# Strassen pairs of a decoder layer: the accumulating DMAs take their second operand from DRAM

## The chip, the cores and the metric

The kernel runs on one core of a Trainium2 chip. Its time is the device time of one execution in microseconds (us); several runs are given as their median. A core has five engines that run side by side: TensorE (PE, with its weight loads PEld), VectorE (DVE), ScalarE (ACT), GpSimd (POOL) and SyncE (SP). SP issues the loads from DRAM here and POOL the accumulating DMAs; both kinds of transfer are carried out by the same 16 DMA engines.

## What is computed

One decoder layer on 256 tokens of width 2048, in float32: a feed-forward half step, a mixer (dilated attention beside gated linear attention), cross-attention to 256 memory tokens, and a second feed-forward half step. The change touches only the two half steps, each of which is

```python
def swiglu(h, w_gate, w_up, w_down):
    return (jax.nn.silu(h @ w_gate) * (h @ w_up)) @ w_down

x = x + 0.5 * swiglu(rms_norm(x, ffn1_norm[l]), ffn1_w_gate[l], ffn1_w_up[l], ffn1_w_down[l])
```

with `w_gate` and `w_up` of 2048 x 5632 and `w_down` of 5632 x 2048. Before it reaches the core, each weight is packed as `W[c, g]`: column block `c` of 512 columns, row group `g` of 512 rows, laid out as a tile of 128 partitions x 4 x 512 (1 MB, 8 KB in a row per partition).

## The kernel before

**Exact products from a split.** Each weight tile `raw` is split into a rounded part `wh` (a cast on ScalarE, L136) and a rest `wl` (a subtraction on VectorE, L137), and so are the activations. A product is three matrix products, `wh` with the high and low part of the activations and `wl` with the high part (`mm3`, L158 to L165; `product`, L188 to L196). `split` is called with the tiles that TensorE will use next, so ScalarE casts, VectorE subtracts and TensorE multiplies, each a tile or two behind the other.

**Half steps.** `ffn` (L346) goes through 11 column blocks `f` in three parts of 4, 4 and 3. Within a part it makes gate and up for each block, then the partial product with `w_down` for all four output columns. The first block of a half step uses the plain `proj`; the other ten use `strassen` (L372), so that the program has 20 calls. The first call of the second and of the third part follows directly on the `w_down` products of the part before; the other calls follow on a gate and up, whose transposition (`turn`, L350, casts at L274, subtractions at L275) is done within the next call.

**A Strassen pair.** `strassen` makes gate and up of a column block together. Its row groups 0 and 1 are the two halves of a 2 x 2 block product of the Strassen-Winograd form, which takes 7 products in place of 8 (each `product` is 12 matrix products on half of the tokens); groups 2 and 3 are plain. The four tiles of groups 0 and 1 are `ral` and `rar` (group `a`, gate and up) and `rbl` and `rbr` (group `b`, gate and up). Sums of them are made in place:

- L229: `ral -> ral + rar` on VectorE (`add`, L210 to L212);
- L230: `rar -> rar + rbr`, an accumulating DMA from POOL (`accumulate`, L214 to L216);
- L235: `ral -> ral + rbr`, so `ral` is now the sum of three, on VectorE;
- L240: `ral -> ral + rbl`, an accumulating DMA once `ral` has been split; the sum of all four is used in the last of the seven products (L252).

In between, `parts` splits the tiles in this order: `ral` as loaded, `ral` with `rar`, `ral` with `rbr` too, `rbl` (L239), `rar` with `rbr` (L241), `rbr` (L244). Then come the left tile of group 2 (`wgroup`, L139), the sum of four in `ral` (L252), and the right tile of group 2, the left and the right one of group 3. ScalarE and VectorE follow that order.

**Buffers and queues.** In the half steps, weight tiles come alternately from two pools of three buffers each (`load`, L121 to L133). A buffer may be written again when every instruction that read the last tile in it is done, and accumulating DMAs count among these. Of the tiles of a call, the left one of group 3 goes to the buffer that `rbr` had, the right one of group 3 to that of `rbl`. All loads are issued from SP, in one fixed order; SP stands still while the next load's buffer isn't free. The load into `rbl`'s buffer is the next one on SP after the right tile of group 2. The framework orders the instructions of each engine at build time, by priority and by when it reckons them ready (`high_priority` moves them ahead) and adds the semaphore waits itself.

Of the kernel before, what the change touches and what calls it, by code (L numbers as in the profile page):

```python
# [49 lines left out]
def layer_kernel(ctx: ExitStack, tc: tile.TileContext, A: dict, out: bass.AP):  # L50
# [23 lines left out]
    def FT(tag, bufs, shape, dt, name):  # L74
        return phase["pool"].tile(shape, dt, tag=tag, name=name, bufs=bufs)

    def W2(shape, name, dt=F32):
        return sp.tile(shape, dt, tag="w", name=name)
# [4 lines left out]
    def PM(shape, name):  # L83
        return pm.tile(shape, F32, tag="ps", name=name)
# [7 lines left out]
    def tick():  # L92
        due = []
        for e in pend:
            e[0] -= 1
            if e[0] <= 0:
                due.append(e)
        for e in due:
            pend.remove(e)
            e[1]()  # L100
# [20 lines left out]
    def load(W, c, g):  # L121

        if wload:
            return wload.pop(0)
        kn, n = W.shape[-2:]
        with tc.high_priority(WPRI):
            phase["loads"] += 1
            if phase["half_step"] and phase["loads"] % 2:
                raw = FT("raw", FRAW, [P, kn, n], F32, "raw")
            else:  # L130
                raw = wp.tile([P, kn, n], F32, tag="raw", name="raw")
            SY.dma_start(raw, W[c, g])
        return raw  # L133

    def split(wh, wl, src):
        SC.copy(wh, src)  # L136
        V.tensor_sub(wl, src, wh.bitcast(F32))  # L137

    def wgroup(W, c, g, fine=None):  # L139

        raw = load(W, c, g)
        n = W.shape[-1]
        kn = W.shape[-2]
        whole = phase["half_step"]
        m = kn if whole else kn // 2
        for h in range(1 if whole else 2):
            with tc.high_priority(WPRI):
                wh, wl = (FT(x, FWB if whole else WB, [P, m, n], F32R, x) for x in ("wh", "wl"))
                for i in range(m if fine else 1):
                    d = slice(i, i + 1) if fine else slice(0, m)  # L150
                    if fine:
                        fine(m * h + i)
                    split(wh[:, d], wl[:, d], raw[:, m * h + d.start:m * h + d.stop])
            ks = [(kn * g + m * h + kk, wh[:, kk], wl[:, kk]) for kk in range(m)]
            for i in range(0, m, kn // 2):
                yield ks[i:i + kn // 2]

    def mm3(acc, lhs, half, first, last, ts=range(TT), seeded=False):  # L158

        for t in ts:  # L160
            for i, (k, wh, wl) in enumerate(half):
                lh, ll = lhs(k, t)
                PE.matmul(acc[t], lh, wh, start=first and i == 0, stop=False, skip_group_check=seeded)  # L163
                PE.matmul(acc[t], lh, wl, start=False, stop=False, skip_group_check=seeded)  # L164
                PE.matmul(acc[t], ll, wh, start=False, stop=last and i == len(half) - 1, skip_group_check=seeded)  # L165
# [22 lines left out]
    def product(acc, lhs, w, start):  # L188

        wh, wl = w  # L190
        first = start
        for i, j, w in ((0, 0, wh), (1, 0, wh), (0, 1, wl)):
            for k in range(4):
                PE.matmul(acc, lhs(k)[i], w[:, k], start=first, stop=j == 1 and k == 3, skip_group_check=not start)  # L194
                first = False
        tick()  # L196

    def strassen(Wl, cl, Wr, cr, lhs, ab, sums, groups):

        a, b = ab  # L200
        ral, rar = load(Wl, cl, a), load(Wr, cr, a)
        rbr, rbl = load(Wr, cr, b), load(Wl, cl, b)

        def parts(src):
            with tc.high_priority(WPRI):
                wh, wl = (FT(x, FWB, [P, 4, 512], F32R, x) for x in ("wh", "wl"))
                split(wh, wl, src)
            return wh, wl

        def add(dst, x, y):  # L210
            with tc.high_priority(WPRI):
                V.tensor_add(dst, x, y)  # L212

        def accumulate(dst, x):  # L214
            with tc.high_priority(WPRI):
                G.dma_start(dst, x, accum_op=ALU.add)  # L216

        def of(g, t):
            return lambda k: lhs(4 * g + k, t)

        def s_(i):
            return lambda k: tuple(x[:, i, k] for x in sums)

        x, y = PM([P, 512], "x"), PM([P, 512], "y")
        c0l, c0r, c1r = (pa.tile([P, 512], F32, tag="acc", name="acc") for _ in range(3))
        product(x, of(a, 0), parts(ral), True)
        with tc.high_priority(WPRI):
            SC.copy(c0l, x)  # L228
        add(ral, ral, rar)  # L229
        accumulate(rar, rbr)  # L230
        product(y, s_(0), parts(ral), True)
        with tc.high_priority(WPRI):
            ys = W2([P, 512], "ys")
            SC.copy(ys, y)
        add(ral, ral, rbr)  # L235
        product(x, s_(1), parts(ral), False)
        with tc.high_priority(WPRI):
            V.tensor_sub(c0r, ys, x)  # L238
        product(c0l, of(b, 0), parts(rbl), False)  # L239
        accumulate(ral, rbl)  # L240
        product(x, s_(2), parts(rar), False)  # L241
        with tc.high_priority(WPRI):
            V.tensor_sub(c1r, ys, x)
        product(c0r, s_(3), parts(rbr), False)  # L244
        accs = ((c0l, x), (c0r, c1r))
        for i, g in enumerate(groups):
            for acc, W, c in zip(accs, (Wl, Wr), (cl, cr)):
                for h, half in enumerate(wgroup(W, c, g)):
                    mm3(acc, lhs, half, False, i == len(groups) - 1 and h == 1, seeded=True)
                    tick()  # L250
                if i == 0 and W is Wl and c == cl:
                    product(x, of(b, 1), parts(ral), False)  # L252
        return accs
# [92 lines left out]
    def ffn(pre, r, after, fine=None, last=False):  # L346
# [18 lines left out]
        for part in PARTS:  # L365
            for f in part:
                if sums is None:
                    gate = proj(wg, f, lhs_x, range(4), fine)
                    if callable(r):
                        r = r()  # L370
                else:
                    gate, upv = strassen(wg, f, wu, f, lhs_x, (0, 1), sums, (2, 3))  # L372
                sg = []
                with tc.high_priority(WPRI):
                    for t in range(TT):
                        s = W2([P, 512], "sg")
                        SC.activation(s, gate[t], AF.Silu, scale=r[:, t:t + 1])
                        sg.append(s)
                if sums is None:
                    upv = proj(wu, f, lhs_x, range(4))  # L380
                hs = []
                with tc.high_priority(WPRI):
                    for t in range(TT):
                        h = W2([P, 512], "h")
                        V.scalar_tensor_tensor(h, upv[t], r[:, t:t + 1], sg[t], op0=ALU.mult, op1=ALU.mult)  # L385
                        hs.append(h)
                later(2, lambda f=f, hs=hs: turn(f, hs))
                if sums is None:
                    sums = tuple(FT(n, 1, [P, 4, 4, P], F32R, n) for n in ("sh", "sl"))
                    with tc.high_priority(WPRI):  # L390
                        sums_of(xT[0], xT[1], lambda i: tuple(p[:, 2 * i:2 * i + 2] for p in sums))
# [643 lines left out]
```

## Time and profile before

| what | value |
|---|---|
| timed runs, median (lowest to highest of 3) | 1957.99 us (1957.59 to 1958.06) |
| profiled execution, span from first to last instruction | 1956.1 us |
| mean granted TensorE clock | 0.995 |
| ACT busy | 988.7 us, 51% |
| loads from DRAM (queue q1) | 370.74 MB, DMA engines busy with them 49.9% of the span |
| accumulating DMAs (queue q0) | 41.95 MB, 10.4% |

The span is the profiled execution's own time; the timed runs take in what lies around it. In rows of the timeline the columns are the start in us, the duration in us, the engine, the line, the operation with output and inputs, the number of instructions merged in the row, and in brackets how long the engine was idle before and what ended that. "SPq" and the DMA rows of POOL are the issuing of a DMA, not its transfer. In a list of waits the columns are the time in total, the number of times, and the longest. In a table of windows they are the stretch, its length, then busy time (and instructions) of PE, PEld, DVE, ACT and POOL, the granted clock, the busy share of the DMA engines and GB/s.

### The profile page before, as it was taken

What the parts mean: (1) busy time and instruction counts of PE and PEld (TensorE: products, weight loads), DVE (VectorE), ACT (ScalarE), POOL (GpSimd) and SP (SyncE); (2) the same over time, 40 slices, a digit from 0 to 9 for tenths busy, and PEclk for the clock granted to TensorE, in tenths of its full rate; (3) what the DMA queues carried; (4) which work ended last, traced back from release to release, by engine and by line L of the source; (5) the groups of instructions that cost most, each with busy time, mean ns of one, the idle gap of its engine ahead of it and who ended that gap; (6) DMA issues with size and microseconds to landing.
All of it is one profiled execution on the core that took longest, in us unless ns stands there. A gap on an engine that the chain in (4) does not pass through costs nothing.

```text
span 1956.1 us, 21465 instructions
## 1 busy us (share of the span) xinstructions
PE 1924.5 (98%) x8760; PEld 1586.4 (81%) x8760; DVE 1270.5 (65%) x1027; ACT 988.7 (51%) x956; POOL 96.1 (5%) x101
## 2 busy tenths in 40 slices
PE   8999999999999999999999999899999999999999
PEld 6888878888878888778888889688887788887887
DVE  6776467775578655546785566777646777457863
ACT  6555345553356446444675446555534555335642
POOL 2000000000000000002230000000000000000000
PEclk9999999999999999999999999999999999999999
DMA  9677547775567725445465554567755777556771
GB/s 368 235 236 258 190 148 264 271 268 192 173 220 237 281 82 186 156 167 191 172 232 207 183 192 151 217 236 233 260 184 146 252 272 274 203 178 215 237 285 59
DMA packets 63294, 416.14 MB, mean 213 GB/s; under 512 B 7099, under 2 KB 8251, under 8 KB 14428
## 3 DMA queue, kind: packets, MB, share of 16 engines
q1 hardware_dynamic: 56284, 370.74, 49.9%
q0 software_dynamic: 5760, 41.95, 10.4%
q10 hardware_dynamic: 1152, 2.10, 0.3%
q8 instruction: 68, 1.11, 0.2%
q14 instruction: 30, 0.25, 0.0%
HBM read 370.72 MB, written 2.10 MB: 191 GB/s over the span
## 4 chain that ended last, share of the span: by engine, by line
PE 74%; DVE 15%; ACT 5%; issue 4%; DMA 1%; POOL 0%; SPq 0%; ACTq 0%; DVEq 0%
PE acc L164 21%; PE acc L165 20%; PE acc L163 20%; DVE wl L137 10%; ACT wh L136 5%; PE x L194 4%; DVE raw L212 4%; PE x L165 1%; PE x L164 1%; PE acc L194 1%; PE x L163 1%; DVE h L385 1%; DMA xr<-in_xT_dram 1%; DVE acc L238 1%; PE y L194 0%
## 5 line engine op out<-in xcount | busy, mean ns | idle before, releaser
L137 DVE TENSOR_TENSOR wl<-raw,wh 128x2048 fp32r<-128x2048 f32 (+2 forms) x487 | 931.5, 1932 | 582.6 <-ACT wh L136 581.8
L136 ACT CAST wh<-raw 128x2048 fp32r<-128x2048 f32 (+2 forms) x487 | 777.0, 1619 | 692.5 <-PE acc L165 503.9
L163 PE MATMUL acc<-wh,xTh 128*128 128x512 f32 x1024 | 402.3, 394 | 16.3 <-ACT wh L136 16.3
L164 PE MATMUL acc<-wl,xTh 128*128 128x512 f32 x1024 | 402.9, 393 | 8.9 <-DVE wl L137 8.9
L165 PE MATMUL acc<-wh,xTl 128*128 128x512 f32 x1024 | 400.5, 391 | 0.0
L163 PE MATMUL acc<-wh,hTh 128*128 128x512 f32 x704 | 274.7, 390 | 0.0
L165 PE MATMUL acc<-wh,hTl 128*128 128x512 f32 x704 | 274.0, 389 | 0.0
L164 PE MATMUL acc<-wl,hTh 128*128 128x512 f32 x704 | 273.9, 389 | 0.0
L163 PEld LDWEIGHTS acc<-wh,xTh 128*128 128x128 f32 x1024 | 192.4, 189 | 59.5 <-ACT wh L136 18.9
L164 PEld LDWEIGHTS acc<-wl,xTh 128*128 128x128 f32 x1024 | 193.3, 189 | 56.9 <-DVE wl L137 17.7
L165 PEld LDWEIGHTS acc<-wh,xTl 128*128 128x128 f32 x1024 | 193.4, 189 | 39.7
L165 PEld LDWEIGHTS acc<-wh,hTl 128*128 128x128 f32 x704 | 132.2, 188 | 27.4
L164 PEld LDWEIGHTS acc<-wl,hTh 128*128 128x128 f32 x704 | 132.2, 188 | 27.2
L163 PEld LDWEIGHTS acc<-wh,hTh 128*128 128x128 f32 x704 | 132.2, 188 | 27.1
L216 POOL DMA_DIRECT2D raw<-raw x40 | 34.6, 864 | 1179.5 <-DVE raw L212 966.9
L212 DVE TENSOR_TENSOR raw<-raw 128x2048 f32<-128x2048 f32 x40 | 91.5, 2288 | 0.7
L165 PE MATMUL x<-wh,xTl 128*128 128x512 f32 x160 | 62.6, 391 | 0.0
L164 PE MATMUL x<-wl,xTh 128*128 128x512 f32 x160 | 62.5, 391 | 0.0
L163 PE MATMUL x<-wh,xTh 128*128 128x512 f32 x160 | 62.4, 390 | 0.0
L228 ACT COPY acc<-x 128x512 f32<-128x512 f32 x20 | 11.4, 571 | 95.6 <-PE x L194 95.6
L396 DVE SCALAR_TENSOR_TENSOR x<-acc,x 128x512 f32<-128x512 f32 x48 | 33.0, 687 | 31.6 <-PE acc L165 31.6
L163 PE MATMUL acc<-wh,mTh 128*128 128x512 f32 x128 | 50.1, 392 | 0.0
(302 smaller groups left out, 1958.9 us busy)
## 6 DMA issues: line engine op xcount, KB each, us to landing
raw<-in_ffn_w_up_dram SPq DMA_DIRECT2D x88, 1024.0 KB, 7.0
raw<-in_ffn_w_down_dram SPq DMA_DIRECT2D x88, 1024.0 KB, 4.9
raw<-in_ffn_w_gate_dram SPq DMA_DIRECT2D x85, 1024.0 KB, 6.9
raw<-in_w_in_dram SPq DMA_DIRECT2D x48, 1024.0 KB, 4.7
raw<-raw POOLq DMA_DIRECT2D x40, 1024.0 KB, 6.9
raw<-in_w_out_dram SPq DMA_DIRECT2D x16, 1024.0 KB, 4.7
raw<-in_xattn_w_k_dram SPq DMA_DIRECT2D x4, 1024.0 KB, 4.8
raw<-in_xattn_w_q_dram SPq DMA_DIRECT2D x4, 1024.0 KB, 5.0
```

The costliest lines, as they stand in the source:

```text
L136: SC.copy(wh, src)
L137: V.tensor_sub(wl, src, wh.bitcast(F32))
L163: PE.matmul(acc[t], lh, wh, start=first and i == 0, stop=False, skip_group_check=seeded)
L164: PE.matmul(acc[t], lh, wl, start=False, stop=False, skip_group_check=seeded)
L165: PE.matmul(acc[t], ll, wh, start=False, stop=last and i == len(half) - 1, skip_group_check=seeded)
L194: PE.matmul(acc, lhs(k)[i], w[:, k], start=first, stop=j == 1 and k == 3, skip_group_check=not start)
L212: V.tensor_add(dst, x, y)
L216: G.dma_start(dst, x, accum_op=ALU.add)
L228: SC.copy(c0l, x)
L238: V.tensor_sub(c0r, ys, x)
L385: V.scalar_tensor_tensor(h, upv[t], r[:, t:t + 1], sg[t], op0=ALU.mult, op1=ALU.mult)
L396: V.scalar_tensor_tensor(xs[c][:, t], acc[t], 0.5, xs[c][:, t], op0=ALU.mult, op1=ALU.add)
```

## The change

The two accumulating DMAs of `strassen` read the second summand from the weight in DRAM, `Wr[cr, b]` and `Wl[cl, b]`. These are the very arrays from which `rbr` and `rbl` were loaded (L202), so that the numbers are the same. The tiles `rbr` and `rbl` are still loaded, as they are split and used in products of their own, and `rbr` in the sum at L235.

```diff
         add(ral, ral, rar)
-        accumulate(rar, rbr)
+        accumulate(rar, Wr[cr, b])
         product(y, s_(0), parts(ral), True)
...
         product(c0l, of(b, 0), parts(rbl), False)
-        accumulate(ral, rbl)
+        accumulate(ral, Wl[cl, b])
         product(x, s_(2), parts(rar), False)
```

## The prediction, made before the changed kernel ran

> **What bounds the kernel now.** I read the page first, then the waits, then the timeline of one Strassen call for each engine.
>
> ```profile
> span 1956.1 us, 21465 instructions
> PE 1924.5 (98%) x8760; PEld 1586.4 (81%) x8760; DVE 1270.5 (65%) x1027; ACT 988.7 (51%) x956; POOL 96.1 (5%) x101
> ...
> raw<-in_w_in_dram SPq DMA_DIRECT2D x48, 1024.0 KB, 4.7
> raw<-raw POOLq DMA_DIRECT2D x40, 1024.0 KB, 6.9
> ```
>
> TensorE has work 98% of the span; 1956.1 - 1924.5 = 31.6 us are all it is idle. An edit that touches only two DMAs per call can gain no more than the part of those 31.6 us that hangs on them. The other rows give the time from issue to landing of 1 MB: 4.7 us for a plain load, 6.9 us for an accumulating DMA, 40 of them in 20 calls of `strassen`.
>
> Who makes TensorE wait, and what the load queue waits for (the list of waits, without and with SP):
>
> ```profile
> PE acc L163 <- ACT wh L136: 16.3, 7, 4.4
> PE acc L164 <- DVE wl L137: 8.9, 18, 3.8
> ...
> SPq L132 <- DMA raw<-raw: 538.8, 20, 27.5
> ```
>
> TensorE waits for the casts and differences of weights, never by name for a DMA. But SP, which issues the weight loads in order, stands once in each of the 20 calls until an accumulating DMA lands. Which one, the timeline of an ordinary call (the one at 300 to 345 us; POOL, SP, DVE, ACT, PE) says:
>
> ```profile
> 314.50 0.85 POOL L216 DMA_DIRECT2D raw<-raw  x1 [31.36 <-DVE raw L212]
> 326.43 0.86 POOL L216 DMA_DIRECT2D raw<-raw  x1 [11.08 <-DVE wl L137]
> ...
> 333.36 0.33 SPq L132 DMA_DIRECT2D raw<-in_ffn_w_up_dram  x1
> 333.79 0.37 SPq L132 DMA_DIRECT2D raw<-in_ffn_w_gate_dram  x1
> ...
> 323.84 4.49 DVE L137 TENSOR_TENSOR wl<-raw,wh 128x2048 fp32r<-128x2048 f32 x2 [2.03 <-ACT wh L136]
> ...
> 333.85 6.69 DVE L137 TENSOR_TENSOR wl<-raw,wh 128x2048 fp32r<-128x2048 f32 x3
> ...
> 325.99 5.53 ACT L136 CAST wh<-raw 128x2048 fp32r<-128x2048 f32 x3
> 331.41 1.07 ACT L274 CAST hTh<-tp 128x512 fp32r<-128x512 f32 x2
> 333.41 3.72 ACT L136 CAST wh<-raw 128x2048 fp32r<-128x2048 f32 x2 [0.93 <-DVE wl L137]
> ...
> 341.35 1.07 PE L194 MATMUL x<-wh,xTh 128*128 128x512 f32 x4
> ...
> 344.07 0.39 PE L163 MATMUL acc<-wh,xTh 128*128 128x512 f32 x1
> ```
>
> The second accumulate (L240, `ral += rbl`) is issued at 326.43 and lands 6.93 us later, at 333.36: at that instant SP issues the next load (into the buffer of `rbl`) and 0.05 us later ScalarE starts the last cast of `ral`. The two casts at 333.41 are that of `ral` and that of the right-hand tile of the next group; TensorE uses them at 341.35 and 344.07. So in an ordinary call the landing has slack. The first accumulate (L230) is issued at 314.50; its result is cast first in the x3 at 325.99, though 314.50 + 6.9 = 321.4: 4.6 us of slack.
>
> In four calls there is none: the first of the second and third part of each feed-forward half. One with its rows, then the waits of TensorE in all four:
>
> ```profile
> 540.85 0.86 POOL L216 DMA_DIRECT2D raw<-raw  x1 [10.66 <-DVE wl L137]
> ...
> 538.26 4.49 DVE L137 TENSOR_TENSOR wl<-raw,wh 128x2048 fp32r<-128x2048 f32 x2 [1.72 <-ACT wh L136]
> ...
> 547.84 0.33 SPq L132 DMA_DIRECT2D raw<-in_ffn_w_up_dram  x1
> ...
> 547.88 3.71 ACT L136 CAST wh<-raw 128x2048 fp32r<-128x2048 f32 x2 [1.94 <-DMA raw<-raw]
> ...
> 293.92 0.73 PE L163 MATMUL acc<-wh,xTh 128*128 128x512 f32 x2 [2.43 <-ACT wh L136]
> ...
> 551.64 0.74 PE L163 MATMUL acc<-wh,xTh 128*128 128x512 f32 x2 [1.59 <-ACT wh L136]
> ...
> 1517.48 0.89 PE L163 MATMUL acc<-wh,xTh 128*128 128x512 f32 x2 [2.42 <-ACT wh L136]
> ...
> 1776.69 0.74 PE L163 MATMUL acc<-wh,xTh 128*128 128x512 f32 x2 [1.50 <-ACT wh L136]
> ```
>
> Here TensorE's fixed order puts the right-hand tile's first product ahead, so it waits at 551.64 for the second of the two casts (547.88 + 3.71 = 551.59), and these wait for the landing. The landing is on TensorE's path four times, with 2.43 + 1.59 + 2.42 + 1.50 = 7.94 us of idle time.
>
> How much a later landing costs can be read from the trace, as two of the four land late already:
>
> ```profile
> 282.29 0.85 POOL L216 DMA_DIRECT2D raw<-raw  x1 [10.66 <-DVE wl L137]
> ...
> 290.12 0.33 SPq L132 DMA_DIRECT2D raw<-in_ffn_w_up_dram  x1
> ...
> 262.50 27.95 SPq L132 DMA_DIRECT2D raw<-in_ffn_w_up_dram  x2
> ```
>
> There it took 290.12 - 282.29 = 7.83 us with 2.43 us of idle, against 6.94 us (540.85 to SP's 547.84, less its 0.05) with 1.59: 0.89 us later, 0.84 us more idle. So 0.94 us of time for each us of delay.
>
> **The change part by part.** Instructions stay: 40 accumulates, the same bytes into the same tiles. Three things move.
>
> (1) *What the accumulates wait for.* They no longer wait for the loads of `rbr` and `rbl`. The waits that end last are others (DVE raw L212, DVE wl L137 in the rows above), so this gives 0. The issue on POOL (0.85 us) has nothing queued behind it in these stages: 0.
>
> (2) *The source.* 40 x 1024 KB = 41.9 MB more are read from HBM. What the transfer itself costs, from the stretches of the accumulate alone and of loads alone:
>
> ```profile
> 326.40:333.40 7.00, 7.00 (x33) 5.77 (x32) 7.00 (x5) 6.08 (x5) 0.86 (x1) 1.00 0.73 150
> ...
> 333.40:341.00 7.60, 7.41 (x33) 5.79 (x32) 7.60 (x5) 3.72 (x2) 0.00 (x0) 1.00 0.86 335
> ```
>
> The last two columns are the share of time that the DMA engines are busy and GB/s. The accumulate keeps them busy 0.73 x 7.00 = 5.1 us for 1.05 MB (150 GB/s x 7.00 us); loads need 0.86 x 7.60 = 6.5 us for 335 x 7.60 = 2.55 MB, 2.6 us for the same size. An accumulate costs the engines twice a load, which is what reading two operands instead of one would cost, wherever they lie. How long it takes from DRAM no row shows. Bounds: 2.6 us, if the DRAM side runs beside the read of the destination as a plain load does; 5.1 + 2.6 = 7.7 us, if the fetch comes on top. I take 5.1, since the cost seems to be one of operands and not of place.
>
> [...]
>
> (3) *What is freed earlier.* This is the part that decides. The buffer of `rbl` is no longer read by the accumulate, so SP's load into it waits only for the difference of `rbl`, the second of the x2 groups: 323.84 + 4.49 = 328.33 in place of 333.36 in the ordinary call, 538.26 + 4.49 = 542.75 in place of 547.84 in the other. SP goes 5 us earlier, and nobody waits for that load: its tile is the last of the call to be cast. The loads behind it wait for other buffers (`rbr`, whose difference ends at about 333.3) and move by 0.4 us. So the early load gains 0. But it now runs beside the second accumulate, where today the DMA engines are left to that alone (150 GB/s in that window is its own 1.05 MB). SP's load is issued 1.9 us after the accumulate. Start and end of a load together take 4.7 - 2.6 = 2.1 us, those of an accumulate 6.9 - 5.1 = 1.8; my estimate is that the starts are 1.0 and 1.4 of these. Then the load's bytes come when about 1.5 of the accumulate's 5.1 us are done and 3.6 us, 70%, remain. If the engines take turns piece by piece, 70% of the load's 2.6 us goes ahead of the accumulate's end: 1.8 us. Bounds: 0, if a transfer once begun is finished first or both run side by side; 2.6, if the whole load passes. I take 1.7, near to taking turns.
>
> *The sum.* The landing comes 1.7 us later in all 20 calls. In 16 it is covered: in the call at 326 us ScalarE would cast `ral` at 335.1 to 337.0 and the next tile to 338.9, needed at 341.35 and 344.07; VectorE's three differences, now back to back to 340.54, would wait 0.9 us after the first and end at 341.4, with the last needed at about 344.3 by the product behind 344.07. That cover holds to a delay of about 4.5 us. In the four calls nothing covers it: 4 x 1.7 x 0.94 = 6.4 us. What is late next there is still the same cast. Against the span 1956.1 + 6.4 = 1962.5; the timed runs have a median of 1957.99, 1.9 us around the span, so 1964.4 us, 0.33% slower.
>
> **The rivals.**
>
> *No cost from sharing (1958).* The accumulate, having begun first, is served first, or the two overlap, or the load is not issued earlier because something else holds it: the change then doesn't do what I read from it. Delay under 1 us, cost under 3.9 us. For it: the engines need not share evenly, and no row here shows a load beside an accumulate. Against: the landing at 290.12 took 7.83 us though SP issued nothing between 262.5 and that landing (the x2 row), so even small other traffic in the DMA engines delays an accumulate.
>
> [...]
>
> *A faster accumulate (1952.6), the other side.* If the read of two operands from one SBUF port is what doubles the cost, a DRAM operand halves the transfer to 2.6 us. Of it 1.5 is done when the load comes; the remaining 1.1 takes turns with 1.1 of the load: 2.2 in place of 3.6, a landing 1.4 us earlier. ScalarE is free for it (1.94 us idle before 547.88), and 4 x 1.4 x 0.94 = 5.3 us come off the 7.94. It decides from a busy time of under about 3.3 us per accumulate (1.5 done, 1.8 left, doubled by the turns: 3.6 as today). Near it stands another order: the instruction order is laid out at build time, and if TensorE's order in the four calls became that of the ordinary ones, most of the 7.94 us would go (about 1951).
>
> *A slower accumulate (about 1979).* At 7.7 us of busy time 80% remains when the load comes, and the landing is 2.6 + 0.8 x 2.6 = 4.7 us late. Four calls: 4 x 4.7 x 0.94 = 18 us; the sixteen others lose the 0.2 us beyond their cover of 4.5, 3 us in all. For it: HBM has to be reached for every piece; against: loads from HBM run at twice the accumulate's rate.
>
> **How the numbers follow.** Forecast (delay 1.05 to 2.6 us, +4 to +10): 0.50. No cost: 0.26. Faster accumulate or other order: 0.15. Slower accumulate: 0.09. A measurement of this kernel tells about 0.2%, 3.9 us, from no change. So faster 0.15, same 0.26, slower 0.59. The likeliest time is 1964.4, its own range 1962 to 1968. The 80% range reaches to the faster accumulate and, above, to 2.6 us of delay with some of the slower transfer: 1952 to 1974; it leaves out most of the slow rival and the far end of the other order.
>
> **What would show it.** Right: SP's load into `rbl`'s buffer issued about 2 us after the second accumulate; that accumulate's landing at 8.3 to 9 us, the first one's still near 6.9; the four idle times of TensorE at 3 to 4 us; nothing new in the sixteen other calls. Wrong: a landing of the first accumulate, which has no load beside it, away from 6.9 (then step 2 fails, by that much); a second landing near 6.9 although the load is early (no sharing); the four idle times gone (another order).

## The result: 16 us slower, half of it through TensorE's clock

| kernel | median | range | ratio to before, 95% interval |
|---|---|---|---|
| before | 1957.79 us | 1957.16 to 1958.06 (4 runs) | |
| changed | 1973.99 us | 1972.54 to 1974.82 (4 runs) | 1.0078 [1.0067, 1.0090] |

The profiled execution of the changed kernel is its fastest run: 1972.54 us, a span of 1970.8 us. The page of its profile (span, busy time, the queue of the accumulating DMAs, and time from issue to landing) and its list of waits:

```profile
span 1970.8 us, 21499 instructions
...
PE 1933.8 (98%) x8760; PEld 1593.3 (81%) x8760; DVE 1272.0 (65%) x1027; ACT 988.0 (50%) x956; POOL 97.9 (5%) x101
...
q0 software_dynamic: 5760, 41.95, 11.6%
...
raw<-in_ffn_w_up_dram POOLq DMA_DIRECT2D x20, 1024.0 KB, 7.9
raw<-in_ffn_w_gate_dram POOLq DMA_DIRECT2D x20, 1024.0 KB, 9.1
...
PE acc L163 <- ACT wh L136: 22.4, 7, 3.9
...
SPq L132 <- DVE wl L137: 1686.6, 327, 21.8
```

The span is 14.7 us longer. TensorE is idle 37.0 us in place of 31.6 (+5.4), and it is *busy* 9.3 us longer with the same 8760 products. More idle time alone doesn't explain the loss: the same work took longer. The landings are both later, 7.9 us for the first accumulate (the `up` weight) and 9.1 for the second (`gate`), against 6.9. SP no longer waits for an accumulating DMA. The rows of the call that the prediction showed at 540 us, now at 543 (POOL, then SP, ScalarE and TensorE):

```profile
542.92 0.86 POOL L216 DMA_DIRECT2D raw<-in_ffn_w_gate_dram  x1 [10.65 <-DVE wl L137]
...
544.85 3.12 SPq L132 DMA_DIRECT2D raw<-in_ffn_w_up_dram  x2
...
552.19 3.70 ACT L136 CAST wh<-raw 128x2048 fp32r<-128x2048 f32 x2 [4.18 <-DMA raw<-in_ffn_w_gate_dram]
...
555.95 1.22 PE L163 MATMUL acc<-wh,xTh 128*128 128x512 f32 x2 [3.79 <-ACT wh L136]
556.96 0.63 PE L164 MATMUL acc<-wl,xTh 128*128 128x512 f32 x1
557.39 0.63 PE L165 MATMUL acc<-wh,xTl 128*128 128x512 f32 x1
```

SP's next load goes out at 544.85, 1.9 us after the accumulate. The cast starts 9.3 us after the accumulate was issued (7.0 before), and TensorE waits 3.79 us in place of 1.59. Behind the wait its products take 0.63 us in place of 0.39. The other three waits of this kind:

```profile
294.48 0.73 PE L163 MATMUL acc<-wh,xTh 128*128 128x512 f32 x2 [3.89 <-ACT wh L136]
...
1527.40 0.73 PE L163 MATMUL acc<-wh,xTh 128*128 128x512 f32 x2 [3.83 <-ACT wh L136]
...
1788.81 1.22 PE L163 MATMUL acc<-wh,xTh 128*128 128x512 f32 x2 [3.78 <-ACT wh L136]
```

Together they are 15.29 us against 7.94: 7.35 us more. The rest is the clock. The windows around the wait, before and after (the column after POOL is the granted clock of TensorE, 1.00 being full speed):

```profile
545.00:550.00 5.00, 5.00 (x23) 3.81 (x21) 5.00 (x4) 3.06 (x3) 0.00 (x0) 1.00 0.62 126
550.00:554.00 4.00, 2.41 (x11) 1.95 (x11) 4.00 (x3) 1.59 (x1) 0.00 (x0) 1.00 1.01 426
554.00:558.00 4.00, 4.00 (x20) 3.29 (x19) 0.97 (x1) 0.54 (x1) 0.00 (x0) 1.00 1.01 420
```

```profile
552.00:556.00 4.00, 0.21 (x2) 0.06 (x1) 2.50 (x2) 3.70 (x2) 0.00 (x0) 0.91 1.01 426
556.00:560.00 4.00, 4.00 (x10) 3.13 (x11) 2.62 (x2) 0.00 (x0) 0.00 (x0) 0.50 1.01 426
560.00:564.00 4.00, 4.00 (x15) 3.17 (x14) 0.00 (x0) 0.00 (x0) 0.00 (x0) 0.74 1.01 424
```

In the first fence the clock stays at 1.00 and 20 products fit into the 4 us behind the wait. In the second it falls to 0.50, and 10 products fit. The clock records of the trace give the slow stretches one by one: in the four calls of the changed kernel they last 3.41, 6.83, 3.41 and 6.83 us (20.5 in all), in those of the kernel before 0, 0, 3.41 and 0. At the granted 0.50 each us of work loses half a us: (20.5 - 3.4) / 2 = 8.5 us, an estimate from these records. Longer waits and slower clock make 15.9 us, less about 1 us for the part of the slow stretches in which TensorE was idle anyway. The small difference that remains to the 14.7 us of the span is in places that the change doesn't touch (the start, and two waits between 1234 and 1246 us), whose idle and slow times also vary from trace to trace.

The sixteen ordinary calls behave as forecast. The landing is later there too, by 1.7 us in the call shown, and ScalarE and VectorE wait for it, but TensorE doesn't (rows of POOL, ScalarE, VectorE and TensorE in the call that was at 326 us):

```profile
328.60 0.86 POOL L216 DMA_DIRECT2D raw<-in_ffn_w_gate_dram  x1 [11.07 <-DVE wl L137]
...
337.24 3.72 ACT L136 CAST wh<-raw 128x2048 fp32r<-128x2048 f32 x2 [2.58 <-DMA raw<-in_ffn_w_gate_dram]
...
339.18 4.49 DVE L137 TENSOR_TENSOR wl<-raw,wh 128x2048 fp32r<-128x2048 f32 x2 [0.88 <-ACT wh L136]
...
338.36 0.50 PE L164 MATMUL acc<-wl,xTh 128*128 128x512 f32 x1 [0.20 <-DVE wl L137]
...
343.48 1.07 PE L194 MATMUL x<-wh,xTh 128*128 128x512 f32 x4
...
346.20 0.39 PE L163 MATMUL acc<-wh,xTh 128*128 128x512 f32 x1
```

The only mark of TensorE waiting is the 0.20 us that the kernel before has too.

### The profile page after: what moved, and what is told of

Its sections match the earlier page's. It is cut to its first block, busy times and chain, and to the rows that moved or that the text cites. A ratio compares the mean times of both kernels' runs of the same rounds, so it can differ in the third digit from the quotient of the medians.

```text
span 1970.8 us, 21499 instructions
## 1 busy us (share of the span) xinstructions
PE 1933.8 (98%) x8760; PEld 1593.3 (81%) x8760; DVE 1272.0 (65%) x1027; ACT 988.0 (50%) x956; POOL 97.9 (5%) x101
## 4 chain that ended last, share of the span: by engine, by line
PE 69%; DVE 16%; issue 6%; ACT 6%; DMA 2%; POOL 0%; SPq 0%; ACTq 0%; POOLq 0%; DVEq 0%
PE acc L164 20%; PE acc L165 20%; PE acc L163 19%; DVE wl L137 10%; ACT wh L136 6%; DVE raw L212 4%; PE x L194 3%; DMA raw<-in_ffn_w_gate_dram 2%; PE x L164 1%; PE x L165 1%; PE x L163 1%; DVE h L385 1%; DVE acc L238 1%; DVE acc L243 1%; PE tp L315 0%
## 5 line engine op out<-in xcount | busy, mean ns | idle before, releaser
L216 POOL DMA_DIRECT2D raw<-in_ffn_w_up_dram x20 | 17.4, 871 | 981.6 <-DVE raw L212 981.6
L396 DVE SCALAR_TENSOR_TENSOR x<-acc,x 128x512 f32<-128x512 f32 x48 | 33.0, 687 | 31.6 <-PE acc L165 31.6
```

The source lines that it names most:

```text
L396: V.scalar_tensor_tensor(xs[c][:, t], acc[t], 0.5, xs[c][:, t], op0=ALU.mult, op1=ALU.add)
```

## The experiments

The theory: the loss is made in the four calls where TensorE waits for the second accumulate's landing. The landing is later for two reasons (source in DRAM, traffic beside it), and behind the longer wait the clock is also halved (0.50 in the window above). Rivals: every accumulate from DRAM costs something; only one of the two reasons matters; the slow clock has another cause. Each run was timed beside the kernel before on the same chip.

### One accumulate at a time

Only L230 changed:

```diff
-        accumulate(rar, rbr)
+        accumulate(rar, Wr[cr, b])
...
         accumulate(ral, rbl)
```

> Only the first accumulate (L230) reads DRAM; the second is as before. Theory (the loss sits in the four calls where TensorE waits for the landing of the second accumulate): the first lands at about 7.9 us in place of 6.9, inside its 4.6 us of slack, and the time is that of before, 1958 +- 2 us. Rival (every accumulate from DRAM costs, wherever it is: 16.2 us over 40 of them): about 1966 us.

Only L240 changed:

```diff
         accumulate(rar, rbr)
...
-        accumulate(ral, rbl)
+        accumulate(ral, Wl[cl, b])
```

> Only the second accumulate (L240) reads DRAM, and the buffer of rbl is free early as in the changed kernel. Theory: the whole loss, 1974 +- 2 us; second landing about 9.1 us, the four waits of TensorE about 3.8 us each. Rival (every accumulate from DRAM costs): about 1966 us.

Measured: the first alone 1958.17 us, ratio 1.0004 [0.9994, 1.0013]; the second alone 1973.17 us, 1.0077 [1.0062, 1.0092]. All of the loss comes from the second accumulate. The rival of a cost per accumulate falls. Landings with the first alone from DRAM:

```profile
q0 software_dynamic: 5760, 41.95, 11.0%
...
raw<-in_ffn_w_up_dram POOLq DMA_DIRECT2D x20, 1024.0 KB, 7.9
raw<-raw POOLq DMA_DIRECT2D x20, 1024.0 KB, 6.9
```

The DRAM source alone makes a landing 1.0 us later (7.9 against 6.9), and it has no load beside it. That is what the first accumulate's slack of 4.6 us hides. The share of queue q0 gives the engines' busy time: 10.4% of 1956.1 us over 40 is 5.1 us per accumulate from SBUF; here 11.0% of 1959.5 us, less 20 x 5.1, over the other 20 is 5.7 us from DRAM.

### No early load

The changed kernel, with a sum of one column on GpSimd behind the second accumulate that reads `rbl` and the new `ral`; its result is not used. It keeps the buffer of `rbl` taken until that sum is done, which is after the landing (in the call near 543 us it waited for the landing until 551.53).

```diff
-        accumulate(ral, Wl[cl, b])
+        accumulate(ral, Wl[cl, b]); G.tensor_tensor(ST(1, "hold"), rbl[:, 0, 0:1], ral[:, 0, 0:1], op=ALU.add)
```

> The changed kernel, with rbl's buffer held until the second accumulate has landed by a one-column sum on GpSimd that reads rbl and the accumulated ral (its result is not used): no weight load beside the accumulate. Theory with two parts of the later landing (1.0 us from the source in DRAM, 1.2 us from sharing the DMA engines): landing about 7.9 us, the four waits 2.5 to 3.4 us, 4 us more than before, and 0 to 5 us more from the clock: 1962 to 1967 us. Rival (sharing alone matters, as predicted): 1958 us. Rival (the DRAM source alone): landing 9.1 us and 1974 us.

Measured: 1965.89 us, 1.0039 [1.0026, 1.0052], between the two. The median landing of both accumulates is near 7.9 us. The fence shows the landings, then SP's loads behind the second accumulate of the call near 543 us (which was issued at 543.37), then the four waits:

```profile
raw<-in_ffn_w_up_dram POOLq DMA_DIRECT2D x20, 1024.0 KB, 8.0
raw<-in_ffn_w_gate_dram POOLq DMA_DIRECT2D x20, 1024.0 KB, 7.9
...
548.10 0.33 SPq L132 DMA_DIRECT2D raw<-in_ffn_w_up_dram  x1
550.30 0.33 SPq L132 DMA_DIRECT2D raw<-in_ffn_w_gate_dram  x1
553.15 0.33 SPq L132 DMA_DIRECT2D raw<-in_ffn_w_up_dram  x1
...
294.76 1.20 PE L163 MATMUL acc<-wh,xTh 128*128 128x512 f32 x2 [2.63 <-ACT wh L136]
...
555.31 0.73 PE L163 MATMUL acc<-wh,xTh 128*128 128x512 f32 x2 [2.78 <-ACT wh L136]
...
1522.68 0.72 PE L163 MATMUL acc<-wh,xTh 128*128 128x512 f32 x2 [2.68 <-ACT wh L136]
...
1782.94 1.17 PE L163 MATMUL acc<-wh,xTh 128*128 128x512 f32 x2 [2.53 <-ACT wh L136]
```

The waits sum to 10.62 us, 2.7 more than before, with slow stretches of 3.41 us behind three of them where there was one: (10.2 - 3.4) / 2 = 3.4 us. That leaves 2 us of the 8 for the varying places. So the source and the traffic each have a part: of the 7.35 us by which the waits grew, 2.7 us come without the early load and 4.7 us with it. One limit: the load into `rbl`'s buffer goes out third here, at 553.15, behind the held sum. Two loads into other buffers still go out before the landing, at 548.10 and 550.30, the first of them 4.7 us behind the accumulate and not 1.9; so a part of the traffic is left in the 2.7.

### No wait for the landing in the four calls

The last of the seven products, with the split of `ral` that it needs, moves behind the right-hand tile of group 2. This changes the order on ScalarE, so that nothing TensorE needs early is queued behind the cast of `ral`. It was run on the changed kernel and on the one before.

```diff
-                if i == 0 and W is Wl and c == cl:
+                if i == 0 and W is Wr and c == cr:
                     product(x, of(b, 1), parts(ral), False)
```

> The changed kernel with the last of the seven products (and the split of the four-fold sum in ral) moved behind the right-hand tile of group 2. In the four calls ScalarE then casts that tile without waiting for the landing. Theory (the four waits and the slow clock behind them are all of the loss): these waits go, in the changed kernel and in the one before alike, so 1950 +- 3 us. Rival (something that touches all twenty calls, as the loads landing later or the new order on SP): at least 1958 us, since only the four waits' lengthening of 7 us would be gone.

> The kernel before (both accumulates from SBUF) with the last of the seven products moved behind the right-hand tile of group 2, as in the run with the changed kernel (1949.1 us). Theory (DRAM source and early load cost nothing where no one waits for the landing): the four waits go here too, 8 us and one slow stretch of 1.7 us, 1948 +- 2 us, within 3 us of that run. Rival (the source costs in ordinary calls too, by less than was seen): at least 4 us faster than that run, 1945 us or less.

Measured: 1949.06 us with the DRAM source, 0.9953 [0.9937, 0.9970], and 1948.92 us with SBUF, 0.9955 [0.9940, 0.9970]. Both are faster than the kernel before and the changed one, and they differ by less than the 3 us that the intervals leave open: where no one waits for the landing, the DRAM source and the early load cost nothing that can be measured here, although the second accumulate still lands late (8.9 us in the first of the two). The lists of TensorE's waits, first with DRAM and then with SBUF, no longer have the four:

```profile
PE acc L163 <- ACT wh L136: 8.4, 3, 4.4
PE acc L164 <- DVE wl L137: 6.3, 5, 3.8
```

```profile
PE acc L163 <- ACT wh L136: 7.7, 3, 3.6
PE acc L164 <- DVE wl L137: 5.4, 4, 3.7
```

The three left are at the start and near 1230 us. So the move was worth 9 us to the kernel before as well. Its four waits of 7.94 us and the one slow stretch behind them are most of that, but not shown to be all: the move touches the sixteen other calls too, where some of TensorE's waits for weight differences go (8.9 us in all become 5.4) and 14 short ones for the difference at L238 come (5.1 us).

### The clock by itself

To part the clock from the wait, TensorE is given something to do in the wait. In the four calls it makes products into the PSUM tile `y`, which nobody reads any more, and the order of the other products is pinned to that of the changed kernel.

```diff
+            for t, acc in enumerate((c0l, x)):
+                PE.matmul(acc, lhs(hl[0][0], t)[0], hl[0][1], start=False, stop=False, skip_group_check=True)
+            for _ in range(12):
+                PE.matmul(y, s_(3)(0)[0], wbr[0][:, 0], start=True, stop=True)
+            pin = PE.matmul(c0r, lhs(hr[0][0], 0)[0], hr[0][1], start=False, stop=False, skip_group_check=True)
...
+                    with tc.issue_after(pin) if done else ExitStack():
```

> The changed kernel, in whose four calls TensorE makes 12 matrix products into a PSUM tile that nobody reads (2.7 us at 0.227 us each) while it waits for the cast; the order of the others is pinned to that of the changed kernel. Theory (idle time of TensorE of about 2 us or more within one 3.41 us window halves its clock for the next window or two): the wait left is 1.1 us, no slow stretch follows in the four calls, and the time falls by some 8 us to 1966 +- 2 us although work was added. Rival (the slow stretches come from something else, as the traffic of the DMA engines, or the idle time alone is the loss): no faster than 1974 us.

Measured: 1973.48 us, 1.0078 [1.0061, 1.0095]. The expectation failed, and the rows say why (ScalarE, then TensorE):

```profile
291.25 1.91 ACT L136 CAST wh<-raw 128x2048 fp32r<-128x2048 f32 x1 [4.28 <-DMA raw<-in_ffn_w_gate_dram]
293.79 1.90 ACT L136 CAST wh<-raw 128x2048 fp32r<-128x2048 f32 x1 [0.63 <-PE y L256]
...
290.87 2.88 PE L256 MATMUL y<-wh,sh 128*128 128x512 f32 x12
295.74 0.50 PE L257 MATMUL acc<-wh,xTh 128*128 128x512 f32 x1 [1.99 <-ACT wh L136]
```

The filling read the very buffer that the awaited cast writes, which held that cast back by 0.63 us. 1.99 us of idle time stayed in one piece, in three of the four calls, and the clock still fell behind each of these. The slow stretches came to 10.2 us in place of 20.5, but counted from the issue of the accumulate the awaited product started 0.8 to 1.8 us later than in the changed kernel, 4.5 us in the four calls together, and that used up the gain. So the run tested the question only in part, but it showed that 1.99 us were enough. With operands that hold no weight buffer, and 14 products:

```diff
-                PE.matmul(y, s_(3)(0)[0], wbr[0][:, 0], start=True, stop=True)
+                PE.matmul(y, s_(3)(0)[0], sums[0][:, 0].rearrange("p a b -> p (a b)"), start=True, stop=True)
```

> As the run before, with 14 products and with operands (the activations' sums) that hold no weight buffer: before, the filling read the buffer that the awaited cast writes, made that cast 0.6 us later and left 1.99 us of idle time in one piece, after which the clock still fell. Theory (idle time within a window of 3.41 us halves the clock): 3.2 us of the 3.8 us wait are filled, about 0.6 us stays idle, no slow stretch follows in the four calls, 8 us less than the changed kernel: 1966 +- 2 us. Rival (the slow clock has another cause): 1972 us or more.

Measured: 1969.53 us, 1.0047 [1.0030, 1.0064]: 56 products were added and the kernel became 4.5 us faster than the changed one by the medians (6 us by the two ratios), where 8 were expected. The waits left, and the clock in the stretches behind the first and the last of them:

```profile
295.85 0.50 PE L257 MATMUL acc<-wh,xTh 128*128 128x512 f32 x1 [0.70 <-ACT wh L136]
...
557.56 0.80 PE L257 MATMUL acc<-wh,xTh 128*128 128x512 f32 x1 [2.45 <-ACT wh L136]
...
1528.16 0.50 PE L257 MATMUL acc<-wh,xTh 128*128 128x512 f32 x1 [1.89 <-ACT wh L136]
...
1789.19 0.50 PE L257 MATMUL acc<-wh,xTh 128*128 128x512 f32 x1 [1.74 <-ACT wh L136]
...
294.00:298.00 4.00, 3.30 (x15) 2.41 (x14) 3.98 (x2) 1.80 (x1) 0.00 (x0) 1.00 1.01 422
...
1790.00:1794.00 4.00, 4.00 (x19) 3.32 (x18) 1.88 (x1) 0.00 (x0) 0.00 (x0) 1.00 1.00 422
```

A slow stretch follows one of the four (2.45 us idle), and none follows the others, although the DMA engines are as busy there as in the changed kernel (1.00 to 1.01). The clock thus goes with the idle time and not with that traffic, as the theory has it. The expected size was missed because in three calls the awaited cast came over a us later than in the changed kernel (3.2 us of filling and 1.7 to 2.5 of waiting, against 3.8); their accumulates landed only after 10.2 to 11.0 us. By the trace's packets 1.2 to 1.5 MB of loads moved between issue and landing there, where it was 0.85 MB in the changed kernel; why more went ahead isn't settled.

## Why the prediction was right, and where it was too small

**What bounds the kernel, and where the change reaches the end: right.** TensorE's four waits for the cast behind the second accumulate were the place. The runs with one accumulate each, and with the last product moved, show it from both sides.

**Step 1 (waits of the accumulates): right**, worth nothing.

**Step 2 (source): too small.** I took the 5.1 us of busy time for both sources; it became 5.7 us, and the landing 1.0 us later. The prediction named this sign: a first landing away from 6.9 us.

**Step 3 (early load beside the accumulate): right in kind, not in its course.** The load went out 1.9 us behind the accumulate as worked out. The delay that it causes was put at 1.7 us; the landing went from 7.9 us (source alone) to 9.1, so 1.2 us. The load's bytes were to come when 30% of the accumulate was done. By the trace's packets in the call at 543 us they began 3.7 us after the load was issued (1.0 us in the kernel before, where nothing else ran), when packets with 70% of the accumulate's bytes had begun. From there 0.7 MB of loads moved ahead of the accumulate's last bytes. That this is the 70% of a load that the prediction had is luck. One more statement was wrong: the loads behind it were to keep their order. The framework put the next `rar` right behind (the x2 row at 544.85), and a third load went out at 549.85, before the landing too. Up to the landing the loads moved 0.85 MB in all, less than the 1.05 MB of one tile; how the 1.2 us divide among them isn't told apart. Sharing with an SBUF source wasn't tried.

Both errors nearly cancel: 2.2 us of later landing in place of 1.7 (1.8 us on average in the four calls, as two of these landed late before), and waits of 3.78 to 3.89 us where 3 to 4 were forecast.

**The step that failed is the price of a us of delay.** "So 0.94 us of time for each us of delay" gave 6.4 us for four waits; they grew by 7.35 us, for 7.3 us of later landings in all, so 1.0 for each us. What was missing is the clock: 8.5 us of slow clock came on top, and the sum had nothing for it. The 0.94 was drawn from two pairs of calls, at 282 and 540 us, behind neither of which the clock fell. The third and the fourth wait of the same fence were not followed. In the kernel before, the rows behind the third say it already:

```profile
1517.48 0.89 PE L163 MATMUL acc<-wh,xTh 128*128 128x512 f32 x2 [2.42 <-ACT wh L136]
1518.16 0.63 PE L164 MATMUL acc<-wl,xTh 128*128 128x512 f32 x1
```

A product of 0.63 us behind a wait of 2.42 us, among products of 0.39: a long wait could have a second price, and the forecast was about to lengthen all four. (The first wait, of 2.43 us, has no such rows; the last section shows why the length alone doesn't decide.) The time of 1973.99 us lies at the very edge of the stated range, whose upper end was meant for other causes: that it lies within is luck.

**The rivals.** No cost from sharing: fell with the landing of 9.1 us. The reason that the prediction gave against it, a landing of 7.83 us put down to other traffic, doesn't hold: the packets show no load beside that accumulate, and why it landed late stays open. A faster accumulate or another order on TensorE: the busy time rose from 5.1 us to 5.7, and TensorE's order is unchanged; why an accumulate from SBUF keeps the engines busy for twice the 2.6 us of a load, no run shows. A slower accumulate: true in part, by 0.6 us of busy time where that rival had 2.6.

## What to carry to other kernels

A buffer that becomes free earlier lets a load go earlier (here 1.9 us behind the accumulate in place of 7.0), and here that load made the transfer beside it land 1.2 us later: ask first whether the transfer it joins is on the path, before counting the early start as harmless. When pricing a longer wait of TensorE, look at the products behind the longest waits that the trace already has; if they are slow there (here 0.63 us in place of 0.39, for 3.41 to 6.83 us), count the wait's length plus, at a clock of 0.50, half of the slow stretch that follows. Moving the work that depends on a late transfer behind work that doesn't (one line here, worth 9 us) paid more than any treatment of the transfer itself that was tried here.

## What the runs showed of the hardware

**When the clock falls.** By the clock records of each profile's trace the slow stretches start at distances that are multiples of 3.413 us from one another, and those that end within the program's run last 3.41, 6.83 or 10.24 us. In the changed kernel they start at 295.86, 555.27, 1241.35, 1528.07 and 1787.49 us: 76, 201, 84 and 76 times 3.4133 us apart. So in these traces the clock changes on a fixed grid of 3.41 us. I cut the nine profiles into windows on that grid, and took those that have over 1.4 us of TensorE idle time and weren't slow already (from 100 us into the span to 1945 us). From the trace's clock records and the ends of its products:

```
idle within one 3.41 us window     windows   clock in the next window
1.42 to 1.87 us                    12        full speed in all
1.99 to 3.26 us                    26        half speed in all
```

So the limit lies between 1.87 and 1.99 us here, 55 to 58% of a window, and whether a wait of 2.4 to 2.8 us passed it depended on how the grid cut it. A wait of 2.78 us split into 1.70 and 1.08 (at 555 us, with the buffer held) left the clock at full speed; 1.99 us in one window did not. In the kernel before, the first of the four waits (2.43 us) is split into 1.42 and 1.01, and the third (2.42 us) lies in one window. That may be part of why the changed kernel's runs spread over 2.3 us; only one of them was traced, so it isn't shown. Once the clock was down, less idle time kept it there: of the slow windows of the nine profiles (from 100 to 1935 us), the 19 with 0.61 to 3.21 us of idle time were followed by another slow one, and the 26 with 0 to 0.59 us by full speed. So the waits that end at 555.95 and 1788.81 us in the changed kernel, 0.67 and 1.32 us into a slow window, bring 6.83 us of slow clock each, and the other two 3.41.

**An accumulating DMA and its source.** With 1 MB and no load beside it, one from DRAM landed 1.0 us later than one from SBUF (7.9 us against 6.9) and kept the engines busy for 5.7 us in place of 5.1; with the second operand in DRAM it isn't halved.
